# The adaLN block with attention and Fourier branches: the residual gate's products gathered in the branch projection, its rows on GpSimd's queue, value products a step later, the latents' combinations after the modulation

## The chip, the cores and the metric

The kernel runs on one NeuronCore of one Trainium2 chip, as one program. The metric is the time of one execution on the device in microseconds, as the median of several runs. The engines are named TensorE (PE, with its weight loads as PEld), VectorE (DVE), ScalarE (ACT), GpSimd (POOL) and SyncE (SP). SP does no arithmetic here: its queue issues most of the loads. ACT and POOL issue transfers of their own from the queues in which their arithmetic stands, in order: what waits at the head of a queue holds back everything behind it.

## The reference

One layer of a diffusion block over 512 latent tokens of width 2048 and 256 context tokens. A conditioning vector c gives shift, scale and gate through one matrix w_ada; the normed latents are modulated with shift and scale; one wide projection w_in gives queries, keys, values, the input of a Fourier mixer, and four sets of gates; the two branches are projected, weighted with sigmoid gates, summed, projected by w_out, and added to the latents under the residual gate.

```python
shift, scale, gate = jnp.split(silu_c @ w_ada[l] + b_ada[l], 3, axis=-1)
h = _modulate(_rmsnorm(xs, norm_g[l]), shift[:, None], scale[:, None])
p = h @ w_l
q = _rope(_rmsnorm(_heads(p, OFF_Q, N_Q_HEADS), q_norm_g[l]), cos, sin) * q_scale
attn = _attention(q, jnp.concatenate([k, kc], axis=1), jnp.concatenate([v, vc], axis=1))
y_a = (attn * jax.nn.silu(z_a)) @ w_pa
y_b = (_fourier_mix(u_b) * jax.nn.silu(z_b)) @ w_pb
y = (g_a * y_a + g_b * y_b) @ w_o
new_xs = xs + gate[:, None] * y
return _rmsnorm(xs, final_g)
```

There are 12 query heads and 4 key/value heads of 128, 768 keys, and everything is float32. The residual gate is the last third of w_ada: 2048 by 2048 numbers, 16 MB, of which each is used once.

## The kernel before, in words

**Products in three parts.** A float32 operand is split into a high part (ACT copies it to fp32r, L141) and a low part (DVE subtracts, L142). mm3 (L266) makes a product of three matmuls: high by high, high by low, low by high (L268 to L270). Weights come as pieces of 128 x 1024 (512 KB): SP loads a raw tile (L177), ACT and DVE split it into whi and wlo, of which three pairs exist, so at most three pieces lie split ahead of TensorE.

**Pieces.** A list `todo` holds all pieces in the order of their use. start_load (L162) takes the first whose raw tiles are free, get (L230) hands a split piece to the products and splits those behind it, split_piece (L207) does the splitting, and, for the large projections, also issues on POOL the accumulating load of the next combination of weights (L224, tiles R).

**Who orders the work.** The code lists the instructions; a planner then fixes the order on each engine's queue before the program runs, by estimated times: on each engine it takes the first instruction in the code's order that is ready by its estimate, so that work that stands later in the code can come earlier in a queue. The helper `issue_after(x)` puts what it encloses behind instruction x on x's engine. Slots (`take`, `give`) are tiles of 4 KB a partition that pass from hand to hand; a transfer into a slot waits for the slot's last reader.

**Stages, in order of time.** The modulation (start to about 178 us): for each of 16 blocks kb of the latents, POOL loads w_ada's shift and scale columns (wa, L390), TensorE multiplies them with the conditioning vector (L474), ACT copies the result (ado, L481), TensorE turns it (L484), DVE makes shift and gain (L490 to L537), and DVE and ACT make the block's high and low parts (make_h, L462 to L464). In between stand matmuls of the first columns of w_in (start_work, L498), whose sums DVE keeps (L506). In the same loop form_row (L546) makes, for each row of blocks j, sums and differences of quadrants of the latents in one tile f (single-buffered) with six small DVE instructions (two at L551, then L554 to L557), and keep_row (L562) writes f to DRAM (f_d) from ACT's queue; the rows are used for a scheme of seven products in place of eight. Row j needs blocks j and j + 8. Then come the Fourier branch (from 201 us on TensorE; its tiles u, fsq, uh take the space of the modulation's tiles), the keys and values, the seven groups of the wide projection, and attention.

**Attention** (about 849 to 1062 us): a loop (L1135) over 48 steps i = 4h + t, h the head, t a block of 128 queries. scores (L1070) makes 128 x 768 scores in PSUM tile x, DVE takes the maximum (L1079), ACT the exponential (L1081) and the scaling of the branch's gate (L1085). turn (L1089) transposes the probabilities of the step before into tp and splits them (pth, ptl). values (L1100) multiplies two steps' probabilities with the values, on odd i from 3 on. load_head (L981) loads the queries of head h + 2 (POOL, from DRAM) and turn_queries (L988) turns and splits those of head h + 1, both at t = 2; get_keys (L985) splits the next keys and values at i = 12g + 8. As filler, products of branch B's projection stand in every step (tile y, L1057).

**The residual gate.** ask_gate (L969) puts a piece of w_ada's gate columns (512 KB, its 1024 rows of c along the free axis) at the head of `todo`; use_gate (L973, L976) multiplies it on DVE with half of the silu of c, spread over all partitions (crow), and sums along the row into one column of gparts. There are 32 pieces, two halves of c by 16 blocks. load_row (L958) loads half of c from ACT's queue, silu_of_row (L962) makes its silu. The first 16 pieces are spread over attention, one in three steps, the other 16 over the steps m of the branch projection. At m = 19 the sums become a column (gcol), which POOL writes to DRAM as a row (gs, L1258); load_rows (L1279) reads it back, spread over the partitions, along with a row of final_g, from ACT's queue (L1282). It is the first job of the output projection.

**The branch projection** (about 1062 to 1215 us): four chunks of 512 columns, each of six steps m of 24 matmuls. The chunks' sums are in PSUM tiles x and y in turn; DVE weights branch B with its sigmoid gate (L1247, the gates loaded by POOL, L1180), and at a chunk's end merges the two (L1261, L1262). turn_merged (L1193, L1199) and form (L1206 to L1213) prepare the output projection's operands as jobs, one a step.

Of the kernel before, what the change touches and what calls it, by code (L numbers as in the profile page):

```python
# [93 lines left out]
def block_kernel(ctx, tc, xT, ctxT, x, c_row, w_ss, w_gate, vecs, qkg, rope, dft_c, dft_s,  # L94
# [111 lines left out]

    def split_piece(e):  # L207
        if e.out is not None or e.kind == "raw":
            return
        raws = [r for _, r in e.raws]  # L210
        src = raws.pop(0) if e.stage is None else chain[e.pc]
        for r in raws:
            nc.vector.tensor_tensor(src, src, r, op=ALU.add)
        if e.off:
            nc.vector.tensor_tensor(src, chain[e.pc], src, op=ALU.subtract)
        hi, lo = e.dst() if e.dst else hl_tiles()
        if isinstance(hi, Halves):
            for k in range(2):
                split_from(src[:, 512 * k : 512 * k + 512].rearrange("p (a c) -> p a c", a=2), hi.parts[k], lo.parts[k])
        else:  # L220
            hi, lo = hi[:, : e.cols], lo[:, : e.cols]
            split_from(src, hi, lo)
        if e.nxt is not None:
            nc.gpsimd.dma_start(chain[e.pc], e.nxt, accum_op=ALU.add)  # L224
# [321 lines left out]
    def form_row(j):  # L546
# [11 lines left out]
        made.append((j, f))  # L558

    made = []  # L560

    def keep_row():  # L562
        j, f = made.pop()
        nc.scalar.dma_start(f_d[:, :, j, :].rearrange("f p c -> p f c"), f)
# [3 lines left out]
    for kb in range(KK):  # L568
# [18 lines left out]
        if kb > 10:  # L587
            keep_row()
        if kb >= 10:
            form_row(kb - 10)  # L590
    for j in (6, 7):
        keep_row()
        form_row(j)
    keep_row()
# [361 lines left out]
    crow = [None]  # L956

    def load_row(half):  # L958
        crow[0] = rp.tile([P, 1024], F32, tag="raw1", bufs=1, name=uid("crow"))
        nc.scalar.dma_start(crow[0], c_row[:, 1024 * half : 1024 * half + 1024].broadcast_to([P, 1024]))  # L960

    def silu_of_row():  # L962

        e = take((1024,))
        nc.scalar.activation(e, crow[0], ACT.Tanh, scale=0.5)
        nc.vector.scalar_tensor_tensor(crow[0], e, 1.0, crow[0], op0=ALU.add, op1=ALU.mult)
# [6 lines left out]
    def use_gate(q):  # L973

        w = get_aside(("gate", q))
        nc.vector.scalar_tensor_tensor(w, w, 0.5, crow[0], op0=ALU.mult, op1=ALU.mult, accum_out=gparts[:, q : q + 1])  # L976
# [57 lines left out]
    load_row(0)  # L1034
# [65 lines left out]
    def values(half):  # L1100
# [8 lines left out]
        if not second:  # L1109
# [4 lines left out]
        if second:  # L1114
# [3 lines left out]
            give(branch.pop(h), qz.pop(h))  # L1118
            if h % GQ == GQ - 1:
                give(*kept.pop(h // GQ))  # L1120
# [61 lines left out]

    m = -1
# [46 lines left out]
    for n, j in enumerate(CHUNKS):  # L1230
# [9 lines left out]
        for pc, t in products(j, accs) if n else first:  # L1240
# [10 lines left out]
            if 3 <= m < 19:  # L1251
                use_gate(KK + m - 3)
            if m < 16:
                ask_gate(KK + m)
            if m == 19:
# [3 lines left out]
                raw_pools.append((rp, 1, "raw1", 1))  # L1259
        for h in range(2):  # L1260
# [18 lines left out]
    def load_rows(g):  # L1279
        for l, src in ((gates, gs.rearrange("(o k) p -> o (k p)", o=1)), (fgs, final_g)):  # L1280
            l[g] = take((2, 512))
            nc.scalar.dma_start(l[g], src[:, 1024 * g : 1024 * g + 1024].broadcast_to([P, 1024]))  # L1282
# [233 lines left out]
```

## Time and profile before

| What | Value |
|---|---|
| Median of 3 runs | 1390.92 us (1390.05 to 1394.07) |
| The profiled execution's own time | 1391.92 us |
| Its span in the profile | 1390.1 us |
| TensorE busy | 1329.1 us, 96% |
| VectorE busy | 983.6 us, 71% |
| ScalarE busy | 674.7 us, 49% |
| GpSimd busy | 136.9 us, 10% |
| Moved by DMA | 294.16 MB, mean 212 GB/s |
| Mean granted TensorE clock | 0.989 |

The profile is one execution. The first part of its page gives each engine's busy time; the second cuts the span in 40 slices of 34.75 us and gives each engine's busy share in tenths. A table by stretches gives, for each stretch, its length and each engine's busy time (with the number of instructions in brackets), then the clock that TensorE was granted, the mean busy share of the 16 DMA engines, and GB/s. A row of the timeline is start, duration, engine, line of the code, operation, tiles written and read, and in brackets how long the engine stood idle before it and what released it. A row of the waits is: who waited for whom, the total in us, how often, the longest. A "q" behind an engine's name (ACTq) is its queue issuing a transfer. Tile names stand without numbers; s is any slot.

### The profile page before, as it was taken

To read this page: it belongs to the slowest core of one execution; us is meant where nothing else is said; L and a number is where in the kernel's file an instruction comes from. 1 tells how busy PE (TensorE), PEld (TensorE's weight loads), DVE (VectorE), ACT (ScalarE), POOL (GpSimd) and SP (SyncE) were. 2 spreads that over 40 slices of the span, in tenths; PEclk is the share of its full clock that TensorE was granted. 3 is DMA by queue.
4 is the path that set the end of the run, shared out by engine and by line. 5 is a ranking of instruction groups with operands and counts; after the bars stand their busy time and mean duration, and the time that the engine had idled before them with its cause. 6 is when DMAs were issued, how large, how long until landed. Compare 5 with 4: busy or idle time off the path is not lost. (4 is left out here: it accounts for less than half of the span.)

```text
span 1390.1 us, 17752 instructions
## 1 busy us (share of the span) xinstructions
PE 1329.1 (96%) x6664; PEld 1079.8 (78%) x6664; DVE 983.6 (71%) x1266; ACT 674.7 (49%) x1036; POOL 136.9 (10%) x188
## 2 busy tenths in 40 slices
PE   7999999999999999999999999899999969999996
PEld 4676788888888888888888887788788748887875
DVE  4776794859888878665666767767666736577777
ACT  5322263447555555545444456666665113354444
POOL 1111000112011211101010100000001000010100
PEclk9999999999999999999999999999999979999999
DMA  9898476859888788878788886424215964378973
GB/s 385 343 365 319 163 231 219 266 179 255 241 224 216 190 249 213 225 267 199 244 191 248 230 247 197 129 62 152 76 31 171 349 206 122 105 159 217 229 213 137
DMA packets 93157, 294.16 MB, mean 212 GB/s; under 512 B 9232, under 2 KB 26128, under 8 KB 88720
## 3 DMA queue, kind: packets, MB, share of 16 engines
q1 hardware_dynamic: 51264, 178.46, 38.5%
q0 software_dynamic: 21168, 91.24, 26.6%
q10 hardware_dynamic: 20640, 23.33, 5.0%
q8 instruction: 52, 0.85, 0.3%
q14 instruction: 33, 0.27, 0.1%
HBM read 265.73 MB, written 27.27 MB: 211 GB/s over the span
## 5 line engine op out<-in xcount | busy, mean ns | idle before, releaser
L141 ACT ACTIVATE whi<-wr 128x1024 fp32r<-128x1024 f32 (+1 forms) x151 | 158.0, 1047 | 234.9 <-PE x L270 74.1
L142 DVE TENSOR_TENSOR wlo<-wr,whi 128x1024 fp32r<-128x1024 f32 (+1 forms) x151 | 181.8, 1207 | 112.1 <-ACT whi L141 111.9
L268 PE MATMUL y<-whi,s 128*128 128x512 f32 x440 | 176.5, 401 | 17.3 <-ACT whi L141 13.0
L269 PE MATMUL x<-wlo,s 128*128 128x512 f32 x476 | 185.8, 390 | 0.6 <-DVE wlo L142 0.5
L268 PE MATMUL x<-whi,s 128*128 128x512 f32 x476 | 186.1, 391 | 0.2 <-ACT s L863 0.2
L270 PE MATMUL x<-whi,s 128*128 128x512 f32 x476 | 185.5, 390 | 0.0
L269 PE MATMUL y<-wlo,s 128*128 128x512 f32 x440 | 173.0, 393 | 2.5 <-DVE wlo L142 2.5
L270 PE MATMUL y<-whi,s 128*128 128x512 f32 x440 | 172.6, 392 | 0.0
L141 ACT ACTIVATE whi<-R 128x1024 fp32r<-128x1024 f32 x96 | 101.5, 1060 | 109.3 <-PE x L270 63.0
L142 DVE TENSOR_TENSOR wlo<-R,whi 128x1024 fp32r<-128x1024 f32 x96 | 116.8, 1221 | 38.8 <-ACT whi L141 38.7
L268 PEld LDWEIGHTS y<-whi,s 128*128 128x128 f32 x440 | 83.3, 189 | 40.5 <-ACT whi L141 13.4
L268 PE MATMUL x<-s,s 128*128 128x512 f32 (+1 forms) x280 | 106.6, 381 | 5.1 <-ACT s L141 4.2
L269 PE MATMUL x<-s,s 128*128 128x512 f32 (+1 forms) x292 | 109.6, 375 | 0.0
L270 PE MATMUL x<-s,s 128*128 128x512 f32 (+1 forms) x292 | 109.4, 375 | 0.0
L269 PEld LDWEIGHTS x<-wlo,s 128*128 128x128 f32 x476 | 89.4, 188 | 19.8 <-DVE wlo L142 1.5
L268 PEld LDWEIGHTS x<-whi,s 128*128 128x128 f32 x476 | 89.4, 188 | 19.1 <-ACT s L863 0.5
L270 PEld LDWEIGHTS x<-whi,s 128*128 128x128 f32 x476 | 89.3, 188 | 18.7
L269 PEld LDWEIGHTS y<-wlo,s 128*128 128x128 f32 x440 | 83.2, 189 | 19.2 <-DVE wlo L142 4.1
L270 PEld LDWEIGHTS y<-whi,s 128*128 128x128 f32 x440 | 83.2, 189 | 17.6
L224 POOL DMA_DIRECT2D R<-in_w_g x56 | 48.7, 875 | 400.0 <-DVE wlo L142 257.3
L141 ACT ACTIVATE s<-wr 128x512 fp32r<-128x512 f32 (+2 forms) x82 | 55.8, 692 | 48.5 <-PE y L270 16.0
L142 DVE TENSOR_TENSOR s<-wr,s 128x512 fp32r<-128x512 f32 (+2 forms) x82 | 61.2, 764 | 23.1 <-ACT s L141 22.6
(282 smaller groups left out, 2640.8 us busy)
## 6 DMA issues: line engine op xcount, KB each, us to landing
wr<-in_w_g SPq DMA_DIRECT2D x112, 512.0 KB, 4.6
wa<-in_w_ss POOLq DMA_DIRECT2D x28, 1024.0 KB, 9.1
R<-in_w_g POOLq DMA_DIRECT2D x56, 512.0 KB, 7.1
wr<-in_w_pab SPq DMA_DIRECT2D x32, 512.0 KB, 4.5
wr<-in_w_gate SPq DMA_DIRECT2D x32, 512.0 KB, 4.1
R<-in_w_g SPq DMA_DIRECT2D x28, 512.0 KB, 4.6
wr<-in_w_kv SPq DMA_DIRECT2D x24, 512.0 KB, 4.2
wr<-in_w_o SPq DMA_DIRECT2D x24, 512.0 KB, 5.3
```

The source lines that it names most:

```text
L141: nc.scalar.activation(hi, src, ACT.Copy)
L142: return nc.vector.tensor_tensor(lo, src, hi.bitcast(F32), op=ALU.subtract)
L224: nc.gpsimd.dma_start(chain[e.pc], e.nxt, accum_op=ALU.add)
L268: nc.tensor.matmul(o, ah, bh, start=start, stop=False, skip_group_check=cont)
L269: nc.tensor.matmul(o, ah, bl, start=False, stop=False, skip_group_check=cont)
L270: nc.tensor.matmul(o, al, bh, start=False, stop=stop, skip_group_check=cont)
```

## The change

Five edits in one diff. The planner is run anew on the whole program.

- The rows' writes: form_row writes f from POOL's queue itself, and keep_row is gone. All eight rows stand behind the loop over kb, each followed by up to six pieces of the remaining start work.
- The residual gate: no piece is asked for in attention. Steps m = 0 to 15 of the branch projection ask for two pieces each, steps 2 to 17 use two each. use_gate's instructions are queued behind the DVE part of the newest split of a weight piece (issue_after on last_split). The column is made at m = 18.
- The rows of c are loaded from POOL's queue: the first half at step 24 of attention, its silu at step 28; the second half into a slot of its own at the start of the branch projection, its silu at m = 2. Both halves are held at once.
- Attention: values at even i from 4 on (a step later), with one more turn of the loop; load_head and turn_queries at t = 1 in place of 2 (a step earlier); get_keys at i = 12g + 10 in place of 12g + 8. The tiles of the head's queries and of a finished key group are given back before the split of the branch's result, no longer after it.
- load_rows issues its two loads from POOL's queue.

```diff
+    last_split = [None]
...
-            split_from(src, hi, lo)
+            last_split[0] = split_from(src, hi, lo)
...
-        made.append((j, f))
-
-    made = []
-
-    def keep_row():
-        j, f = made.pop()
-        nc.scalar.dma_start(f_d[:, :, j, :].rearrange("f p c -> p f c"), f)
+        nc.gpsimd.dma_start(f_d[:, :, j, :].rearrange("f p c -> p f c"), f)
...
-        if kb > 10:
-            keep_row()
-        if kb >= 10:
-            form_row(kb - 10)
-    for j in (6, 7):
-        keep_row()
+    for j in range(8):
         form_row(j)
-    keep_row()
+        for _ in range(6):
+            next(work, None)
     pa.close()
...
-    crow = [None]
+    crow = [None, None]
 
     def load_row(half):
-        crow[0] = rp.tile([P, 1024], F32, tag="raw1", bufs=1, name=uid("crow"))
-        nc.scalar.dma_start(crow[0], c_row[:, 1024 * half : 1024 * half + 1024].broadcast_to([P, 1024]))
+        row = crow[half] = take((1024,)) if half else rp.tile([P, 1024], F32, tag="raw1", bufs=1, name=uid("crow"))
+        nc.gpsimd.dma_start(row, c_row[:, 1024 * half : 1024 * half + 1024].broadcast_to([P, 1024]))
...
-        nc.vector.scalar_tensor_tensor(w, w, 0.5, crow[0], op0=ALU.mult, op1=ALU.mult, accum_out=gparts[:, q : q + 1])
+        with tc.issue_after(last_split[0].ins):
+            nc.vector.scalar_tensor_tensor(w, w, 0.5, crow[q // KK], op0=ALU.mult, op1=ALU.mult,
+                                           accum_out=gparts[:, q : q + 1])
...
-        if not second:
+        if second:
+            give(qz.pop(h))
+            if h % GQ == GQ - 1:
+                give(*kept.pop(h // GQ))
+        else:
             branch[h] = take((2, T))
...
-            give(branch.pop(h), qz.pop(h))
-            if h % GQ == GQ - 1:
-                give(*kept.pop(h // GQ))
+            give(branch.pop(h))
...
-    for i in range(NSTEP + 2):
+    for i in range(NSTEP + 3):
         h, t = divmod(i, 4)
         if i < NSTEP:
-            if t == 2 and h + 2 < NH:
+            if t == 1 and h + 2 < NH:
                 load_head(h + 2)
-            if i == 4:
-                silu_of_row()
-            if i % 12 == 8 and i // 12 + 1 < NKV:
+            if i == 24:
+                load_row(0)
+            elif i == 28:
+                silu_of_row(0)
+            if i % 12 == 10 and i // 12 + 1 < NKV:
                 get_keys(i // 12 + 1)
...
-        if i % 2 == 1 and i >= 3:
-            values((i - 3) // 2)
+        if i % 2 == 0 and i >= 4:
+            values((i - 4) // 2)
         if 1 <= i <= NSTEP:
             turn(i - 1)
-        if i % 3 == 2 and i < NSTEP:
-            if i > 2:
-                use_gate(i // 3 - 1)
-            ask_gate(i // 3)
-        if t == 2 and h + 1 < NH:
+        if t == 1 and h + 1 < NH:
             turn_queries(h + 1, b1())
...
-        if i >= NSTEP - 1:
+        if NSTEP > i - 2 >= NSTEP - 3:
             next(first)
             next(first)
-    use_gate(KK - 1)
-    load_row(1)
-    silu_of_row()
...
+    load_row(1)
     m = -1
...
-            if 3 <= m < 19:
-                use_gate(KK + m - 3)
+            if m == 2:
+                silu_of_row(1)
+            if 2 <= m < 18:
+                for i in range(2):
+                    use_gate(2 * (m - 2) + i)
             if m < 16:
-                ask_gate(KK + m)
-            if m == 19:
+                for i in range(2):
+                    ask_gate(2 * m + i)
+            if m == 18:
...
+                give(crow[1])
...
             l[g] = take((2, 512))
-            nc.scalar.dma_start(l[g], src[:, 1024 * g : 1024 * g + 1024].broadcast_to([P, 1024]))
+            nc.gpsimd.dma_start(l[g], src[:, 1024 * g : 1024 * g + 1024].broadcast_to([P, 1024]))
```

More of the change, by code (lines that the diff above doesn't have):

```diff
@@ L953, in qz_done, with silu_of_row @@
                                 r[:, b])
-    crow = [None]
+    crow = [None, None]
     def load_row(half):
-        crow[0] = rp.tile([P, 1024], F32, tag="raw1", bufs=1, name=uid("crow"))
-        nc.scalar.dma_start(crow[0], c_row[:, 1024 * half : 1024 * half + 1024].broadcast_to([P, 1024]))
[L962 to L966, printed above, removed]
+        row = crow[half] = take((1024,)) if half else rp.tile([P, 1024], F32, tag="raw1", bufs=1, name=uid("crow"))
+        nc.gpsimd.dma_start(row, c_row[:, 1024 * half : 1024 * half + 1024].broadcast_to([P, 1024]))
+    def silu_of_row(half):
+        e, row = take((1024,)), crow[half]
+        nc.scalar.activation(e, row, ACT.Tanh, scale=0.5)
+        nc.vector.scalar_tensor_tensor(row, e, 1.0, row, op0=ALU.add, op1=ALU.mult)
         give(e)
@@ L1033, in block_kernel @@
     assert not any(p[0] is gvp or p[2] == "raw1" for e in ahead for p, _ in e.raws)
-    load_row(0)
     ybs, S = {}, {}
```

## The prediction

> **What bounds the kernel now.** First the page: the busy shares and the slices.
>
> ```profile
> span 1390.1 us, 17752 instructions
> PE 1329.1 (96%) x6664; PEld 1079.8 (78%) x6664; DVE 983.6 (71%) x1266; ACT 674.7 (49%) x1036; POOL 136.9 (10%) x188
> PE   7999999999999999999999999899999969999996
> ```
>
> TensorE is busy 96% of the span, so only its idle time, 1390.1 - 1329.1 = 61 us, can be won or added to. One slice, the 33rd, stands out. Next the table by stretches, with TensorE's busy time first and the granted clock, DMA share and GB/s last.
>
> ```profile
> 125.00:150.00 25.00, 21.20 (x112) 16.34 (x111) 17.19 (x34) 5.00 (x6) 1.06 (x2) 0.93 0.78 295
> 1075.00:1100.00 25.00, 23.83 (x106) 19.39 (x105) 15.53 (x20) 5.30 (x5) 2.11 (x4) 1.00 0.99 381
> 1125.00:1150.00 25.00, 11.53 (x39) 8.61 (x38) 8.21 (x7) 5.92 (x7) 1.20 (x1) 0.66 0.60 165
> 849.00:1062.00 213.00, 199.25 (x1270) 169.57 (x1268) 148.06 (x234) 139.09 (x264) 4.23 (x8) 1.00 0.33 103
> 1141.80:1147.80 6.00, 5.53 (x12) 4.05 (x13) 5.97 (x6) 3.82 (x4) 0.00 (x0) 0.50 0.46 136
> 141.70:152.70 11.00, 11.00 (x48) 8.78 (x50) 7.66 (x15) 1.91 (x3) 0.00 (x0) 0.88 0.49 167
> ```
>
> Three places hold what the diff can reach: one stall near 1130, 13.5 us of idle; one near 139, 3.8 us; and attention, 849 to 1062, where 213.0 - 199.25 = 13.8 us are scattered in pieces. Third, the timeline around the big stall, by engine.
>
> ```profile
> 1125.36 1.20 POOL L1258 DMA_DIRECT2D gs<-gcol  x1 [4.77 <-DVE gcol L1257]
> 1111.57 1.08 ACT L1199 COPY s<-x 128x512 f32<-128x512 f32 x2 [1.22 <-PE x L1193]
> 1139.33 0.33 ACTq L1282 DMA_DIRECT2D s<-gs  x1
> 1139.69 1.07 ACT L1199 COPY s<-x 128x512 f32<-128x512 f32 x2 [27.04 <-DMA gs<-gcol]
> 1140.65 1.07 ACT L141 ACTIVATE whi<-wr 128x1024 fp32r<-128x1024 f32 x1
> 1141.78 0.79 PE L268 MATMUL y<-whi,s 128*128 128x512 f32 x1 [13.01 <-ACT whi L141]
> ```
>
> ScalarE's queue holds the load of the residual gate's row (L1282), which waits for the write of that row to DRAM (L1258, issued at 1125.36, landed 13.9 us later). The load belongs to the output projection's code, whose first accumulating load is issued at 1211.47 (row below), some 72 us later, but it stands in the queue ahead of the splits of the branch projection's weights. ScalarE does nothing for 27.0 us, TensorE uses up the split weights and stops for 13.4 us (0.4 of it counts as the end of a matmul).
>
> **Part 1, the gate's row on GpSimd's queue.** ScalarE no longer waits at L1282: the 13.4 us go. After the stall the granted clock is 0.50 for 6.0 us (row above), which costs 3.0 us more. Sum 16.4, I take **16**. The Trainium skill's "TensorE: Matmul & The Clock Gate" (What's actually happening) has the array throttled by default and released by about 3.4 us of sustained work; an estimate by it is 1.7 us in place of 3.0, and the trace shows a longer slow stretch.
>
> Next: who pays for the wait on GpSimd? Behind L1282 on that queue stand loads of sigmoid gates (L1180) and accumulating weight loads (L224).
>
> ```profile
> 1185.35 0.53 POOL L1180 DMA_DIRECT2D s<-g_d  x1 [29.84 <-DVE s L1262]
> 1211.47 0.88 POOL L224 DMA_DIRECT2D R<-in_w_o  x1 [25.59 <-DVE wlo L142]
> ```
>
> GpSimd has 25 to 30 us between its last issues. The write of the row now comes from step 18 of 24 of the projection (below), 33 us before its end; less 14 us for the landing and 7 for the loads themselves, the row is there 12 us before the projection ends, and L224's first issue is later than that. Nothing is late next; a queue blocked 14 us longer would cost 0 to 2.
>
> **Part 2, the combinations of the latents (form_row, L546).** The rows move behind the modulation loop in the code, and their eight writes go from ScalarE's to GpSimd's queue.
>
> ```profile
> 137.58 0.69 DVE L551 TENSOR_TENSOR f<-s,s 128x512 f32<-128x512 f32 x1 [5.44 <-DMA f_d<-f]
> 140.95 0.37 ACT L481 COPY ado<-pd 128x256 f32<-128x256 f32 x1 [5.90 <-DVE f L557]
> 141.38 0.69 PE L484 MATMUL pd<-ident,ado 128*128 128x128 f32 x2 [3.80 <-ACT ado L481]
> L551 DVE TENSOR_TENSOR f<-s,s x16: 681/692/693, 26.2 to 172.0; 128x512 f32<-128x512 f32 x16
> DMA to landing us min/median/max: 2.9/4.3/9.7
> 177.47 1.06 ACT L141 ACTIVATE fsq<-wr 128x1024 fp32r<-128x1024 f32 x1 [2.49 <-DMA f_d<-f]
> 201.10 0.28 PE L268 MATMUL pb<-fch,uh 128*128 128x256 f32 x1
> ```
>
> The only buffer f is written out (9.7 us), VectorE waits for it, ScalarE's queue waits for VectorE with the write of the next row, and the modulation's copy (L481) waits behind it: TensorE stops 3.8 us. Then the granted clock is 0.88 for 11.0 us: 1.3 more. Both go, 5.1. Against it: the stage that follows begins when the last row has landed (177.47).
>
> ```profile
> R<-in_w_g POOLq DMA_DIRECT2D x56, 512.0 KB, 7.1
> R<-in_w_g SPq DMA_DIRECT2D x28, 512.0 KB, 4.6
> ```
>
> The same 512 KB into the same tiles land 2.5 us later from GpSimd's queue (part of that is the accumulation). The last row then lands near 180. TensorE needs the stage's first tiles at 201.10, and VectorE is busy 23.2 of 25 us there, so 0 to 3 us come back; I take 1.5. Net gain **3.5**. The eight rows' arithmetic itself (2.6 us each) stays on VectorE in any case. "DMA: Bandwidth & Descriptors" of the Trainium skill (SWDGE vs HWDGE vs iDMA) speaks against this edit: a transfer issued by GpSimd has its descriptors written by software into SBUF, which VectorE can lock out, and one issued by ScalarE has not. The rows above agree in sign, and GpSimd's issues stay at 0.53 us under a busy VectorE.
>
> Are the rows really computed later? The first L551 ran at 26.2, though its code stands after the modulation of step 10, near 90: the planner takes what is ready. So I expect the rows where they are, paced by their inputs.
>
> **Part 3, attention.** Sixteen gate products (L976) and their 16 loads leave it; value products, the next head's queries and the keys shift by one or two steps.
>
> ```profile
> L976 DVE SCALAR_TENSOR_TENSOR wr<-wr,crow 128x1024 f32<-128x1024 f32 x17 | 20.8, 1223 | 8.7 <-DMA wr<-in_w_gate 8.7
> PE x L268 <- ACT s L141: 4.2, 5, 1.1
> PE y L269 <- DVE ptl L142: 2.9, 6, 0.8
> PE y L268 <- DVE s L1113: 1.9, 6, 0.6
> PE tp L1093 <- DVE ptl L142: 1.2, 3, 0.8
> ```
>
> VectorE is relieved of 16/17 of 20.8 + 8.7 us of work and waits, 28 us of 213. Scores waiting for split queries (4.2) get one step more, 4.4 us; value products waiting for split probabilities (2.9) likewise. The last two rows shrink only if VectorE's relief reaches them. Bounds: nothing, or all 13.8; below nothing too, since keys are split two steps before use instead of four. I take **6** of 13.8, most of the first two rows.
>
> **Part 4, the branch projection** gets 32 gate products in place of 16, two at a step, pinned behind the newest weight split on VectorE.
>
> ```profile
> 1080.58 1.06 ACT L141 ACTIVATE whi<-wr 128x1024 fp32r<-128x1024 f32 x1 [4.38 <-PE x L270]
> 1086.02 1.06 ACT L141 ACTIVATE whi<-wr 128x1024 fp32r<-128x1024 f32 x1 [4.38 <-PE x L270]
> 1104.83 1.23 DVE L976 SCALAR_TENSOR_TENSOR wr<-wr,crow 128x1024 f32<-128x1024 f32 x1
> 1105.98 1.22 DVE L1262 TENSOR_TENSOR R<-s,R 128x1024 f32<-128x1024 f32 x1
> 1107.12 1.22 DVE L1261 TENSOR_TENSOR s<-x,s 128x1024 f32<-128x1024 f32 x1
> L976 DVE SCALAR_TENSOR_TENSOR wr<-wr,crow 128x1024 f32<-128x1024 f32 x15 | 18.4, 1224 | 9.8 <-DMA wr<-in_w_gate 9.8
> ```
>
> A step is 1086.02 - 1080.58 = 5.44 us, a chunk of six 32.7. VectorE per chunk: 12 products at 1.15 and 6 splits, 2 branch-B and 4 merging products at 1.14, together 27.5, and up to 5 form instructions (5.7): 33.2, as much as there is. DMA per chunk: 12 gate pieces, 6 weight pieces, 4 sigmoid gates of 0.524 MB; at the 381 GB/s that the stretch from 1075 shows, 1.38 us each, 30.3 of 32.7. Both are just enough, and the work is not urgent: three split weights lie ready (two steps, 10.9 us), and a gate piece is asked for two steps ahead. Without that cover: the waits now are 9.8/15 = 0.65 us a product, 12 of them 7.8 a chunk, over two full chunks 15.6, less 10.9 of lead: 5 us. For nothing speaks that the products now run ahead of the splits and that two waits of 1.2 us at splits and merges come from that. I take **0**, bounds -2 and +8. The row's two silu products (L965, L966) stay two.
>
> **Sum**, against the profiled execution's own 1391.92 (1390.1 span, 1.8 around it): 1391.92 - 16 - 3.5 - 6 - 0 = 1366.4, I say **1366**. The runs' median is 1.0 lower, within their spread.
>
> **Rivals.** (a) The projection pays: VectorE or DMA is the bound in chunks 0 to 2, by the waits of 0.65 us. 5 to 8 us back: 1371 to 1375, and with a poor attention 1380. For it: 33.2 of 32.7 us. Against: the lead of two steps, and chunk 3, which has no products.
> (b) Writes from GpSimd's queue land later, the skill's rule: with 2.5 to 5 us more for each of seven rows, VectorE, which idles 7 to 8 of 25 us there, waits up to 35 us more before the single f; the modulation comes late and part 2 gains nothing or loses 5: 1370 to 1375. For it: the loads of the modulation's weights stand on the same queue.
> (c) Slower: the planner keeps the rows behind the modulation, as the code has them. Then eight rows run one after another from 172 on, each 2.6 us of VectorE and a landing of 4.3 to 7.1 in the single buffer, 7 to 10 us, the last landing at 228 to 250 in place of 177.5. The stage that starts at 177.47 has 201.1 - 177.5 = 23.6 us of cover, of which it needs some 10; the rest, 37 to 60 us, is a stall: 1403 to 1426, say 1413. It decides once the last landing is later than about 190. Against: 26.2 above, and L1282, pulled ahead by some 72 us.
> (d) The change does not do what it says: the row's wait on GpSimd's queue holds sigmoid gates or L224, and half or all of the 16 us stay: 1374 to 1382.
>
> **How the numbers follow.** Forecast 62% (1357 to 1374: attention between 13 and nothing, part 2 between 5 and 1), (a) 13%, (b) 9%, (c) 8%, (d) 5%, and 3% for an order of the queues that makes no difference. The range 1354 to 1386 takes in the forecast with its tails, (a), (b) and (d), and leaves out (c) and the 3%, with some tail for what I have not thought of. Faster by over 0.3% (below 1386.7; 0.3% is about what a measurement of this kernel tells from no change): 62 + 13 + 9 + 5, less 4 for tails: 0.85. Same 0.05, slower 0.10.
>
> **What would show it.** Right: no idle slice at 1130; ScalarE without a wait for gs; no 5.9 us wait of L481 for f; PE's wait for "ACT s L141" in attention near zero; L976 only after attention. Wrong: L551 all after 172 and the tile fsq waiting on f_d (c); VectorE's wait for in_w_gate above 15 us with PE waiting for wlo (a); POOL's wait for gs with a late L1180 or L224 (d).

## The result, and the profile after

The changed kernel takes 1356.86 us (median of 4 runs, 1354.84 to 1359.74) beside 1392.49 us of the kernel before on the same chip: a ratio of 0.9744, with a 95% interval of 0.9716 to 0.9773, or 36 us less. The forecast was 1366 with a range of 1354 to 1386: the time lies in the range, 9 us below the forecast, and just under the 1357 to 1374 that the forecast's own 62% had named. The profiled execution is the slowest of the four, 1359.74 us.

The page of the kernel after, its span, TensorE's busy time and TensorE's slices:

```profile
span 1358.0 us, 17733 instructions
PE 1319.7 (97%) x6664; PEld 1078.9 (79%) x6664; DVE 983.8 (72%) x1266; ACT 672.8 (50%) x1036; POOL 145.6 (11%) x202
PE   6999999999999999999999999999999999999996
```

No slice stands out any more: the 33rd had a 6. The same 6664 matmuls have 38.3 us of idle time around them in place of 61, and, which the forecast had not thought of beyond the half clock, 9.4 us less busy time.

To see where it went I cut both traces at the same events: the first maximum of attention (L1079), the last high-by-high matmul of the projection's chunk 0 in tile x, and the first and last one of chunk 2 (chunk 1 is summed in tile y between them). Times in us, one profiled execution each:

| Stage | before | after | difference | forecast |
|---|---|---|---|---|
| start to the first maximum of attention | 850.1 | 852.9 | +2.8 | -3.5 |
| attention and chunk 0 | 246.3 | 232.8 | -13.5 | -6 |
| chunk 1 (with the big stop) | 54.2 | 34.7 | -19.5 | -16 |
| chunk 2 | 34.2 | 34.2 | 0 | 0 |
| from the end of chunk 2 on | 205.2 | 203.3 | -1.9 | 0 |

Rows of the table by stretches of the kernel after: first the place of the old stop of the start, then the two stages that changed.

```profile
125.00:150.00 25.00, 25.00 (x151) 19.11 (x153) 16.90 (x30) 6.56 (x9) 2.77 (x5) 1.00 0.91 342
852.90:1085.70 232.80, 226.11 (x1429) 196.89 (x1428) 152.64 (x229) 147.85 (x276) 10.00 (x19) 1.00 0.28 101
1085.70:1120.40 34.70, 34.70 (x163) 28.91 (x162) 30.54 (x38) 10.21 (x12) 2.11 (x4) 1.00 0.90 332
```

The same two stages of the kernel before:

```profile
850.10:1096.40 246.30, 232.31 (x1429) 196.96 (x1428) 169.83 (x264) 147.92 (x275) 9.49 (x18) 1.00 0.41 135
1096.40:1150.60 54.20, 38.37 (x162) 30.34 (x161) 30.78 (x36) 10.18 (x12) 3.31 (x5) 0.84 0.73 225
```

In chunk 1 TensorE is never idle any more, at full clock, with the DMA engines busy 90% of the time. In attention 1429 matmuls at full clock have 6.7 us of idle time in place of 14.0, and 6.2 us less busy time.

GpSimd's timeline of the kernel after shows the write of the gate's row, its load, and what stands behind it on the queue:

```profile
1166.48 1.20 POOL L1253 DMA_DIRECT2D gs<-gcol  x1 [5.83 <-DVE gcol L1252]
1177.37 0.54 POOL L1278 DMA_DIRECT2D s<-gs  x1 [9.69 <-DMA gs<-gcol]
1181.18 0.88 POOL L226 DMA_DIRECT2D R<-in_w_o  x1 [3.27 <-DVE wlo L142]
```

The wait of 9.69 us is now GpSimd's, and the accumulating load behind it (L226) waits afterwards for VectorE, not for the row. The 32 gate products, in VectorE's groups between 1065 and 1165 us (busy, mean ns, idle time before them):

```profile
L969 DVE SCALAR_TENSOR_TENSOR wr<-wr,crow 128x1024 f32<-128x1024 f32 x16 | 19.0, 1221 | 1.0 <-DMA wr<-in_w_gate 1.0
L969 DVE SCALAR_TENSOR_TENSOR wr<-wr,s 128x1024 f32<-128x1024 f32 x16 | 19.0, 1221 | 0.8 <-DMA wr<-in_w_gate 0.8
```

Twice as many products as before, with 1.8 us of waits in place of 9.8.

### The profile page after: what moved, and what is told of

It is laid out like the page before. It is cut to its first block, busy times and chain, and to the rows that moved or that the text cites. A ratio compares the mean times of both kernels' runs of the same rounds, so it can differ in the third digit from the quotient of the medians.

```text
span 1358.0 us, 17733 instructions
## 1 busy us (share of the span) xinstructions
PE 1319.7 (97%) x6664; PEld 1078.9 (79%) x6664; DVE 983.8 (72%) x1266; ACT 672.8 (50%) x1036; POOL 145.6 (11%) x202
## 5 line engine op out<-in xcount | busy, mean ns | idle before, releaser
L141 ACT ACTIVATE whi<-R 128x1024 fp32r<-128x1024 f32 x96 | 101.5, 1060 | 109.0 <-PE x L272 64.4
L271 PEld LDWEIGHTS y<-wlo,s 128*128 128x128 f32 x440 | 82.7, 188 | 15.2
L226 POOL DMA_DIRECT2D R<-in_w_g x56 | 48.8, 875 | 400.2 <-DVE wlo L142 258.2
```

Of the source, the lines that this page charges most:

```text
L141: nc.scalar.activation(hi, src, ACT.Copy)
L271: nc.tensor.matmul(o, ah, bl, start=False, stop=False, skip_group_check=cont)
```

## The experiments

**Theory at the start.** Each of the four parts removes what the prediction says, and the parts add up. **First rival**, suggested by the two rows above: two paced products at a step bring the gate's column in time, so that the load of the row would stop nobody on either queue; then the queue edit is worth nothing in the changed kernel. **Second rival**, for attention: its gain is VectorE's relief and not the shift of the value products.

All kernels compute the whole reference. Differences in us are the ratio to the kernel before, less one, times 1392.5.

| Kernel | Median us (runs) | Ratio, 95% interval | Difference |
|---|---|---|---|
| after | 1356.86 (4) | 0.9744, 0.9716 to 0.9773 | -35.6 |
| e1: before, load_rows on GpSimd's queue | 1379.09 (6) | 0.9899, 0.9877 to 0.9921 | -14.1 |
| e2: before, the residual gate's part alone | 1368.07 (4) | 0.9825, 0.980 to 0.985 | -24.4 |
| e3: after, load_rows back on ScalarE's | 1356.61 (5) | 0.9744, 0.9719 to 0.9769 | -35.6 |
| e4: before, the attention shift alone | 1377.39 (6) | 0.9894, 0.987 to 0.9919 | -14.8 |
| e8: before, value products a step later | 1380.34 (4) | 0.9904, 0.9888 to 0.992 | -13.4 |
| e10: before, queries turned a step earlier | 1389.3 (12) | 0.9972, 0.996 to 0.9985 | -3.9 |
| e5: before, the rows' part alone | 1390.57 (12) | 0.9981, 0.9968 to 0.9994 | -2.6 |
| e6: after, the rows' part undone | 1359.22 (4) | 0.9751, 0.9733 to 0.9769 | -34.7 |
| e9: after, gate products not pinned | 1370.14 (5) | 0.9821, 0.9803 to 0.984 | -24.9 |
| e12: e9, load_rows on ScalarE's queue | 1378.33 (4) | 0.9891, 0.9871 to 0.9911 | -15.2 |
| e11: after, keys at their old step | 1356.77 (5) | 0.9736, 0.9715 to 0.9757 | -36.8 |
| e13: after, the rows in halves | 1351.12 (5) | 0.969, 0.9667 to 0.9712 | -43.2 |

### e1 and e2: two ways to lose the same stop

e1 is the queue edit alone:

```diff
-            nc.scalar.dma_start(l[g], src[:, 1024 * g : 1024 * g + 1024].broadcast_to([P, 1024]))
+            nc.gpsimd.dma_start(l[g], src[:, 1024 * g : 1024 * g + 1024].broadcast_to([P, 1024]))
```

> The kernel before, with one edit: the two loads of load_rows come from GpSimd's queue. My theory (ScalarE's queue holds the splits back behind the wait for gs, nothing else): TensorE's 13 us stop near 1130 and the half clock after it are gone, about -16 us (ratio about 0.988), and the wait for gs appears on GpSimd without a late sigmoid gate or accumulating load. Rival 1 (the loads behind it on GpSimd take the stall over): VectorE waits at L1247 or L224 is late, half or more of the 16 us stay. Rival 2 (the stall is worth more than its gap, because what follows was put off with it): more than -20 us.

e2 is the residual gate's part alone (the hunks of load_row, silu_of_row, use_gate, last_split and the steps m of the projection); load_rows stays on ScalarE's queue:

```diff
+        with tc.issue_after(last_split[0].ins):
...
-            if i > 2:
-                use_gate(i // 3 - 1)
-            ask_gate(i // 3)
...
+                for i in range(2):
+                    use_gate(2 * (m - 2) + i)
```

> The kernel before, with the residual gate's part of the change alone: 32 products in the branch projection behind the newest split, rows of c from GpSimd's queue, both halves held; attention's steps, form_row and load_rows as before (the row of the gate still on ScalarE's queue). If VectorE's relief is what attention gains from: attention 8 to 12 us shorter, and TensorE in the projection without waits at wlo (3 us). If the shift of the values and queries is what it gains from: attention at most 3 us shorter. On the stall: if the queue is its cause, ScalarE still waits for gs and TensorE still stops, 5 to 16 us; if the early gate products are its cause (the column is made 12 us after ScalarE stands at the load), the stop is nearly gone. Together -10 to -30 us.

e1 gives -14.1, chunk 1 shrinks by 16.8 to 37.4 us at full clock, and TensorE has no stop of more than 1.3 us there. (In e1's profile attention and chunk 0, which the edit doesn't touch, took 2.8 us more than before: VectorE waited 3.3 us for one gate piece near 974, ahead of a step that TensorE needed.) GpSimd's timeline of e1:

```profile
1129.57 1.20 POOL L1258 DMA_DIRECT2D gs<-gcol  x1 [4.64 <-DVE gcol L1257]
1145.18 0.54 POOL L1282 DMA_DIRECT2D s<-gs  x1 [14.41 <-issue]
1145.71 0.53 POOL L1180 DMA_DIRECT2D s<-g_d  x1
```

The queue is held for 14.41 us and a sigmoid gate's load stands behind it; VectorE waits 7.8 us for that gate until 1154.84, TensorE never waits in consequence. That is the prediction's part 1, to the letter. But e2 gives -24.4 with the load still on ScalarE's queue, and there too chunk 1 is 34.7 us with TensorE busy throughout. ScalarE's wait in e2 (who waited for it, total, times, longest):

```profile
ACT whi L141 <- DMA gs<-gcol: 8.0, 1, 8.0
```

It was 27.0 us in the kernel before. A wait of 8.0 us is less than the 10.9 us that two split pieces last. Attention and chunk 0 also fall, to 239.1 us, 7.2 less: between the 8 to 12 that the expectation had for VectorE's relief and the 3 at most for the shift, so neither is the whole of it. Whether the 7.2 come from the products' work or from the waits for their loads, no run separates.

### e3: the queue edit undone in the kernel after

```diff
-            nc.gpsimd.dma_start(l[g], src[:, 1024 * g : 1024 * g + 1024].broadcast_to([P, 1024]))
+            nc.scalar.dma_start(l[g], src[:, 1024 * g : 1024 * g + 1024].broadcast_to([P, 1024]))
```

> The changed kernel, with load_rows back on ScalarE's queue; TensorE's order of instructions is the same in both. Queue theory: ScalarE waits for the landing of gs, some 8 to 10 us, ahead of a weight split, and TensorE stops for the part that the two split pieces do not cover, with half clock after it: 3 to 16 us slower than the changed kernel. Pacing theory: the wait is short enough for the cover of 10.9 us: within 2 us of the changed kernel, and the queue edit was not needed once the products are paced.

1356.61 us, the ratio of the kernel after to the fourth digit. The write in GpSimd's timeline of e3, then the load in ScalarE's:

```profile
1161.88 1.20 POOL L1253 DMA_DIRECT2D gs<-gcol  x1 [5.83 <-DVE gcol L1252]
```

```profile
1173.08 0.33 ACTq L1278 DMA_DIRECT2D s<-gs  x1
1173.51 1.06 ACT L141 ACTIVATE whi<-wr 128x1024 fp32r<-128x1024 f32 x1 [9.50 <-DMA gs<-gcol]
```

ScalarE begins to wait at 1173.51 - 9.50 = 1164.0, 2 us after the write was issued: it waits for the landing and for nothing else, 9.5 us, and TensorE lives on split pieces meanwhile. In the kernel before it began at 1139.69 - 27.04 = 1112.65, 13 us before the write was issued. So the stop had two halves: a load that stood in its queue 13 us before its data was written, and a landing of 14 us. The other kernels with this load on ScalarE's queue show how much of such a wait the split pieces cover. Waits of 27.0 us (before), 25.2 (e8), 25.0 (e4), 24.8 (e5), 24.3 (e10) and 18.4 (e12) left TensorE stops of 13.0, 9.5, 9.6, 10.8, 10.2 and 3.5 us; waits of 9.5 (e3) and 8.0 (e2) left none. The stop is the wait less 14 to 16 us, so the cover was longer than the 10.9 us that the prediction counted. That either half alone would be covered is an estimate from these rows: it would just fit, and no run has a wait between 9.5 and 18.4 us. In the changed kernel the queue edit is worth nothing that the runs can tell: in e3 chunks 1 and 2 take 34.7 and 34.2 us, as in the kernel after.

### e9 and e12: what keeps the column in time

e9 takes the pin off:

```diff
-        with tc.issue_after(last_split[0].ins):
-            nc.vector.scalar_tensor_tensor(w, w, 0.5, crow[q // KK], op0=ALU.mult, op1=ALU.mult,
-                                           accum_out=gparts[:, q : q + 1])
+        nc.vector.scalar_tensor_tensor(w, w, 0.5, crow[q // KK], op0=ALU.mult, op1=ALU.mult, accum_out=gparts[:, q : q + 1])
```

> The changed kernel without the order that puts each gate product behind the newest weight split. If the pin is what keeps the projection free of waits: products run ahead again, VectorE waits for gate pieces ahead of splits and merges, TensorE waits at wlo and the column is early; with load_rows on GpSimd's queue no long stop: +2 to +5 us against the changed kernel. If two products a step are pace enough by the raw tiles that they need: within 1 us of it.

1370.14 us: 13 us over the kernel after, far more than the expectation had. Chunk 1 takes 44.8 us (+10.1), attention with chunk 0 236.6 (+3.8). VectorE's waits in e9 between 1060 and 1165 us, its timeline at one stop, and TensorE's timeline there:

```profile
DVE wr L968 <- DMA wr<-in_w_gate: 12.8, 6, 4.5
DVE wlo L142 <- ACT whi L141: 5.9, 2, 3.3
DVE s L1236 <- DMA s<-g_d: 4.3, 1, 4.3
```

```profile
1117.13 0.08 DVE L968 DVE_READ_ACCUMULATOR wr<-wr,s 128x1 f32 x1
1121.47 1.22 DVE L1236 TENSOR_TENSOR s<-s,s 128x1024 f32<-128x1024 f32 x1 [4.26 <-DMA s<-g_d]
1122.61 1.22 DVE L142 TENSOR_TENSOR wlo<-wr,whi 128x1024 fp32r<-128x1024 f32 x1
```

```profile
1123.88 0.80 PE L271 MATMUL y<-wlo,s 128*128 128x512 f32 x1 [5.01 <-DVE wlo L142]
```

Products run before the splits. A wait of VectorE for a transfer (12.8 us for gate pieces, 4.3 for a sigmoid gate) then stands ahead of the split that TensorE needs: the split of 1122.61 had its input since 1114.3, when ScalarE finished the piece's high part, but its queue is in order. With the pin the split comes first, the waits for gate pieces are 1.8 us in all, and they and the 4.2 us for sigmoid gates fall on work that nobody waits for.

e12 is e9 with load_rows on ScalarE's queue as in e3. It tells whether the pace or merely the number of products a step made e3 harmless.

> The kernel after without the pin of the gate products behind the splits and with the row's load back on ScalarE's queue. Pinned, the queue made no difference. The pacing theory: without the pin VectorE meets waits for gate pieces and the gate column comes later than the planner's estimate, so the load stands at ScalarE ahead of its data, for longer than two split pieces last (10.9 us): a stop of 3 to 12 us beyond the version with no pin and GpSimd's queue (1370), 1373 to 1382. The rival, that two products at a step alone keep the column in time whatever their order: 1370 within 2 us, and ScalarE waits 10 us or less for gs.

1378.33 us, 8 over e9, as the pacing theory has it. GpSimd's row and ScalarE's row:

```profile
1145.46 1.20 POOL L1251 DMA_DIRECT2D gs<-gcol  x1 [29.47 <-DVE gcol L1250]
```

```profile
1155.97 1.07 ACT L1188 COPY s<-y 128x512 f32<-128x512 f32 x2 [18.39 <-DMA gs<-gcol]
```

ScalarE begins to wait at 1137.6, 8 us before the write is issued, TensorE stops 3.5 us for the split behind it, and chunk 2 grows from 34.2 to 40.6 us. So the same two lines of load_rows cost 14 us, 8 us or nothing, by how well VectorE keeps the time that the planner reckoned with. That the planner's estimate leaves out VectorE's waits for pieces is argued from this, not shown.

### e4, e8, e10, e11: the parts of the attention shift

e4 has the whole shift, with no gate product moved. e8 has of it the later value products and the earlier give:

```diff
-    for i in range(NSTEP + 2):
+    for i in range(NSTEP + 3):
...
-        if i % 2 == 1 and i >= 3:
-            values((i - 3) // 2)
+        if i % 2 == 0 and i >= 4:
+            values((i - 4) // 2)
```

> The kernel before, with the steps of attention alone shifted (values a step later, head loads and queries a step earlier, keys two steps later, tiles given back earlier), gate products as before. If the shift is what attention gains from: the waits of scores for split queries (4.2 us) and of value products for split probabilities (2.9 us) are nearly gone, attention 6 to 9 us shorter, and the stall near 1130 stays: -5 to -9 us. If VectorE's relief is the cause: attention at most 3 us shorter, or longer, since sixteen gate products and their waits stay on VectorE.

> The kernel before, with the value products alone a step later (even steps from 4 on, one more turn of the loop, tiles given back earlier); queries, heads and keys as before. The whole shift gave 246.3 to 235.9 us from attention's first maximum to the end of the projection's first chunk. If the value products are the cause: most of these 10 us, and the wait for split probabilities (2.9 us) gone. If the earlier queries are: 3 us or less, and the wait of scores for split queries (4.2 us) stays or grows, since queries and value products now stand in one step and share a PSUM bank. The stop near 1130 stays.

e10 has only the other end, on the kernel before; e11 takes the keys back to their old step in the kernel after:

```diff
-        if t == 2 and h + 1 < NH:
+        if t == 1 and h + 1 < NH:
             turn_queries(h + 1, b1())
```

```diff
-            if i % 12 == 10 and i // 12 + 1 < NKV:
+            if i % 12 == 8 and i // 12 + 1 < NKV:
```

> The kernel before with one edit: the next head's queries are turned at t = 1 of a head in place of t = 2. It parts the attention shift, of which the whole is worth some 15 us and the value products alone some 13. If queries and values are independent gains, this gives 1 to 3 us (ratio 0.998 to 0.999), and TensorE's wait of the scores for the split queries (4.2 us, 5 times in the kernel before) goes. If instead any step of slack in attention heals most of its stops, because the stops pass from one place to the other, it gives 6 us or more (0.996 or less). If the queries are only the place where a late VectorE shows, it gives nothing and the wait returns as one for ptl or for the exponential.

> The kernel after with one edit undone: the next keys are split at step 12g + 8 again, not 12g + 10. No product waits for keys in either trace, so both theories have it at 1357 within 1 us; if the two steps mattered for VectorE's load around them, the stops for ptl and for the exponential (5 us together) change by up to 2 us, to 1355 or 1359.

e4 -14.8, e8 -13.4, e10 -3.9, and e11 the same as the kernel after. Attention and chunk 0: 246.3 us before, 235.9 in e4, 237.7 in e8, 245.4 in e10. e4's gain is well beyond the 5 to 9 us that were expected. The step of the value products is worth 8.6 of e4's 10.4 us in attention; the rest of their gains is in chunk 1, where the stop is shorter (9.6 and 9.5 us). The second rival, that VectorE's relief is the whole gain, is wrong: the shift alone gives 10.4, the relief alone (e2) 7.2, and both together 13.5, less than their sum, so in part they heal the same stops. TensorE's waits between 850 and 1060 us in e4, in the kernel after, and then the scores' wait alone in e8 and in e10 (there from 845 to 1170 us):

```profile
PE tp L1093 <- DVE ptl L142: 3.8, 5, 1.3
PE x L268 <- ACT s L1081: 3.0, 4, 0.8
PE x L268 <- ACT s L141: 1.0, 1, 1.0
```

```profile
PE tp L1086 <- DVE ptl L142: 2.8, 4, 1.0
PE x L270 <- ACT s L1074: 2.2, 3, 0.8
PE x L270 <- ACT s L141: 1.4, 1, 1.4
```

```profile
PE x L268 <- ACT s L141: 4.8, 9, 1.0
```

```profile
PE x L268 <- ACT s L141: 5.4, 8, 1.1
```

The scores' wait for the split queries goes (4.2 to 1.0 us) only where queries and value products have both moved. In e10 it did not go although the queries are turned a step earlier: the expectation was wrong there, and the gain of e10 stands in chunk 1 (50.8 us) and not in attention. Why, the runs don't settle: the profile of e5, whose edit ends at 180 us, has 51.9 us in chunk 1, so a single profile of that stage moves by 2 us or more, and the 3 us that e4, e8 and e10 gain in chunk 1 may be no more than that.

### e5, e6 and e13: the rows of the latents' combinations

e5 is that part alone, e6 the kernel after without it. Both carry the diff's hunks of form_row, keep_row and the loop, forwards and backwards:

```diff
-        if kb > 10:
-            keep_row()
-        if kb >= 10:
-            form_row(kb - 10)
-    for j in (6, 7):
-        keep_row()
+    for j in range(8):
         form_row(j)
```

> The kernel before, with form_row's part alone: the eight rows behind the modulation loop, their writes from GpSimd's queue. My forecast: ScalarE's wait for the row and the 3.8 us stop near 139 with its slower clock are gone, up to 3 us come back at the start of the Fourier stage: -3.5 us, attention begins near 846 to 848 (850.1 before). Rival 1: what the queue releases is lost where the next stage waits for the last row's landing: between -1 and +1, attention begins at 850 to 854 as in the kernels with the rows in place (850.1, 852.5, 853.6, 850.1). Rival 2: rows run only after the loop: +37 us or more.

> The changed kernel with form_row and keep_row as before (rows in the loop, writes from ScalarE's queue). If the rows' edit gains 3.5 us, this is 3 to 4 us slower than the changed kernel, near 1360; if it gains nothing, 1356 to 1358; if it costs, it is the fastest so far, near 1353. Attention and later as in the changed kernel: from attention's first maximum to the end of the projection's first chunk 232.8 us.

e5 gives -2.6 us (-4.5 to -0.8 by its interval); e6 is 1 us above the kernel after by the ratios, within their intervals. A better measure of so small a gain: seven profiles have the old start (before, e1, e2, e4, e6, e8, e10; 850.1 to 853.6 us to the first maximum of attention, mean 852.1) and six the new one (after, e3, e5, e9, e11, e12; 848.0 to 852.9, mean 850.3). So the part is worth about 1.9 us. The two groups overlap: by their spread the gain lies between 0 and 3.8 (an estimate, 95%), so the 3.5 of the forecast is less likely, not excluded. In the kernel after the tile f shows where the gain went, then VectorE's timeline and TensorE's:

```profile
L553 DVE TENSOR_TENSOR f<-s,s x16: 681/692/694, 25.5 to 173.7; 128x512 f32<-128x512 f32 x16
...
  DVE f L553: 11.4, 7
...
DMA to landing us min/median/max: 3.5/5.4/14.7
```

```profile
163.64 0.69 DVE L553 TENSOR_TENSOR f<-s,s 128x512 f32<-128x512 f32 x1 [2.04 <-DMA f_d<-f]
...
168.70 0.75 DVE L464 SCALAR_TENSOR_TENSOR ht<-xt,gain,rx 128x512 f32<-128x512 f32 x1
```

```profile
170.26 0.50 PE L270 MATMUL pb<-s,whi 128*128 128x512 f32 x1 [2.70 <-ACT s L465]
```

The rows run from 25.5 to 173.7, where they ran before. ScalarE no longer waits for f, but the one buffer is still there: VectorE waits for it 11.4 us in 7 waits, and the 2.04 us at 163.64, with the row's own work, stand ahead of the last block's modulation (L464), for whose parts TensorE stops 2.70 us. All six profiles with the new start have this stop, 2.3 to 2.8 us. The wait has moved from ScalarE's queue to VectorE's.

This pointed to a version that might be better than both. A second f does not fit into the space, but a row needs only two tiles of 128 x 512 if its last two combinations are made in place, and three such tiles take the space of f and its helper:

```diff
-        f = pap.tile([P, 4, 256], F32, tag="f4", bufs=1, name=uid("f4"))
-        v = pap.tile([P, 2, 256], F32, tag="f2", bufs=1, name=uid("f2"))
+        f, v = (pap.tile([P, 2, 256], F32, tag="f2", bufs=3, name=uid("f2")) for _ in range(2))
...
-        nc.gpsimd.dma_start(f_d[:, :, j, :].rearrange("f p c -> p f c"), f)
+        nc.gpsimd.dma_start(f_d[0:2, :, j, :].rearrange("f p c -> p f c"), f)
+        nc.gpsimd.dma_start(f_d[2, :, j, :], s2)
+        nc.gpsimd.dma_start(f_d[3, :, j, :], s4)
```

> The kernel after, with the rows of the latents' combinations in halves: a row needs two tiles of 128 x 512 in place of three (its last two combinations are made in place), and three such tiles stand where f and its helper stood, so that a row can begin before the whole of the row before has landed. Three writes a row in place of one. If the single buffer f still costs time in the kernel after (VectorE waits 11.4 us in 7 waits for f's write, and two of them, 2.0 us each, stand ahead of a modulation that TensorE waits 2.7 us for), VectorE's waits for f fall below 5 us and the time by 1 to 4 us, to 1353 to 1356. If the start is bound elsewhere, TensorE's stops only change their place: 1357 within 1 us. If 16 more writes on GpSimd's queue land later than one large one, the stage behind the rows starts later: 1358 to 1361.

1351.12 us, 0.969 of the kernel before (0.9667 to 0.9712), 5.7 us below the kernel after by the medians and 7.5 by the ratios: more than the 1 to 4 that were expected, though VectorE's waits for f are not below 5 us. VectorE's wait for f in e13, and the stretch from 125 to 175 us in e13:

```profile
DVE f L552 <- DMA f_d<-f: 6.5, 4, 3.0
```

```profile
125.00:175.00 50.00, 49.98 (x293) 38.33 (x291) 39.25 (x75) 12.46 (x16) 10.21 (x17) 1.00 0.68 241
```

The same stretch of the kernel after, whose work stands at the same point at 125 us (as many matmuls from 50 us on in both, 552):

```profile
125.00:175.00 50.00, 47.30 (x281) 35.90 (x280) 36.27 (x67) 11.93 (x16) 5.04 (x8) 1.00 0.65 235
```

The waits for f fall from 11.4 to 6.5 us, TensorE's stops in this stretch go (2.7 us of idle to none), 12 more matmuls are done in it, and attention begins at 846.0, earlier than in any other profile here (4.3 us before the mean of the six with the new start). The later stages take what they take in the kernel after (232.7, 34.7, 34.2 and 203.0 us).

The profiles can also be laid side by side by the number of the matmul, since TensorE's order up to attention is the same in e13 and the six with the new start, and differs at 7 places in the others. From the 760th to the 1000th matmul, where the old stop was, the seven profiles with the old start take 4.1 to 8.3 us longer than e13, the six with the new start 0.0 to 0.3. From the 1000th to the 1040th, where the stop behind VectorE's wait for f is, the six take 2.7 to 4.3 us longer than e13. Part of this is the clock: in the kernel after it stayed at 1.00 behind the stop of 2.70 us, in e3 it was 0.59 for 4 us behind one of 2.75.

## Why the prediction was right or wrong, point by point

**Part 1, 16 us: the size was right, the cause was one of two.** Alone the queue edit takes 16.8 us off chunk 1 and 14.1 off the whole (e1), TensorE pays nothing for what stands on GpSimd's queue, and the granted clock of 0.50 behind the stop went with it: chunk 1 runs at 1.00. But the step costed the edit against the kernel before, as if the other parts left the stop as it was. Part 4 removes the same stop by itself (e2), and beside it the queue edit is worth nothing (e3). The sum came out because the stop was counted once; with part 4 costed by itself it would have been counted twice.

**Part 2, 3.5 us: right in sign, about 1.9.** The 5.9 us wait of the copy and its 3.8 us stop are gone, as "both go, 5.1" says. What failed is the list of who is late next: VectorE's own wait for f, quoted in that part, was left out of it, and TensorE's stop behind it gave back 2.7 us in the kernel after and up to 4.3 in the other five profiles with the new start. Rival (b) named this wait. The landings did become later, 5.4 and at most 14.7 us in place of 4.3 and 9.7, in sign as the Trainium skill's "DMA: Bandwidth & Descriptors" (SWDGE vs HWDGE vs iDMA) has it, which gives the faster setup to transfers that ScalarE or SyncE issues. VectorE's wait for f grew by only 0.8 us, from 10.6 (the tile's view of the kernel before) to 11.4, so that rival's price of up to 35 us was far off.

**Part 3, 6 us: the term that was mis-sized, it is 13.5 with chunk 0.** The step's bound was "nothing, or all 13.8", the idle time that the busy column leaves. Idle time did fall by 7.3 us, near the 6 taken, and mostly in the two rows that it named: the scores' wait for split queries fell from 4.2 to 1.4 us, the values' wait for split probabilities from 2.9 to none. But the stage gained nearly as much again out of the busy column. The timeline of TensorE in the kernel before shows how busy time can hide a stop:

```profile
895.74 0.50 PE L268 MATMUL y<-whi,s 128*128 128x512 f32 x1 [0.34 <-DVE s L1113]
896.07 0.39 PE L269 MATMUL y<-wlo,s 128*128 128x512 f32 x1
896.29 0.39 PE L270 MATMUL y<-whi,s 128*128 128x512 f32 x1
897.36 0.33 PE L990 MATMUL y<-ident,s 128*128 128x128 f32 x1 [0.68 <-ACT R L1057]
```

Matmuls of 512 columns start 0.23 us apart when nothing is late, but each is on record for 0.39. When the next one is late, the first 0.16 us of that count as busy: 897.36 is 1.07 us behind its predecessor, 0.84 late, and the profile shows 0.68. The starts give the whole loss, as an estimate from this case's own paces: where nobody waits, the next matmul starts 0.227 us after one of 512 columns, 0.118 after one of 256 and 0.109 after a transpose of 128. At these paces the stage's matmuls need 217 us, so it lost 29 us before and 16 after, 13.5 less, which is the whole difference; the idle column has only 14.0 and 6.7 of it. (In chunk 1 of the kernel after, where TensorE never waits, the same paces leave nothing lost.) So the true upper bound of this part was nearer 29 than 13.8.

**Part 4, 0: it gave 2.7 beside part 1, and alone it would have given part 1's gain as well (e2).** Of chunk 1's 19.5 us 16.8 go with the queue edit alone (e1); the other 2.7 are the small waits for splits and merges (1.6 and 1.2 us before), which the step named and gave nothing for. The bounds were -2 and +8. The reason against a loss, that products no longer run ahead of the splits, was right and undervalued: without the pin it is 13 us (e9) where the step had 5. And a chunk is longer than the step's 32.7 us, for it left out the transposes: at full clock it takes 34.2 to 34.7, of which VectorE is busy 30.5 and 32.7, so VectorE had room. Rival (a) is much like what e9 shows; that e9's 1370 us stands beside its 1371 to 1375 is luck, since e9 loses 13 us where the rival had 5 to 8, from a kernel 9 us below the forecast.

**Rivals (c) and (d)** did not occur: L553 runs from 25.5 on, and L226 is not held by the row.

**The sum again**, with what was measured: 1391.9 - 16.8 - 1.9 - 13.5 - 2.7 - 1.9 (the last stage, which no step had) = 1355.1, beside the median of 1356.9. The profiled execution is longer, for its start is the longest of the six with the new start.

## What to carry to other kernels

A load that waits in an arithmetic engine's queue costs nothing as long as the work split ahead outlasts it. What makes it expensive is standing there before its data is computed, so first look when the wait begins and when the write that it waits for is issued, then decide whether to move the load or to pace the producer, and cost two edits that heal the same stop together. Pin the work that may be late behind the work that another engine needs, and read TensorE's loss from the distances of its starts, for the busy column swallows the first part of every stop. When a wait for a single buffer is moved to another engine, it is still there; writing the row in halves, in the same space, took 5.7 us off a kernel in which the order of the queues had taken 2.

## What the runs showed of the hardware

- The write of the gate's column, 2048 numbers that land as single elements (8 KB), took long in every profile: the load could be issued 14.0 us after it in the kernel before, 10.9 in the kernel after, 11.2 in e3, and 9.5 to 15.6 in all fourteen. A write of 512 KB in rows of 1 KB from the same queue had a median of 5.4 us. The Trainium skill's "DMA: Bandwidth & Descriptors" (Specifications) names 512 B as the least transfer for line rate, and (Anatomy of one DMA) a fixed cost of about 2 us; the trace agrees with the first in kind, and the time is several times the second.
- A short stop of TensorE can cost more than itself: behind a stop of 2.3 to 2.8 us at the same place of six kernels the granted clock stayed at 1.00 in one profile (after) and fell in the other five (0.59 for 4 us in e3).
- The start stage of one and the same code differed by up to 5 us between executions (848.0 to 852.9 in the profiles of six kernels), so a part worth 2 us cannot be read from one profile.
- 24 smaller writes in e13 did not land later than 8 large ones: a median of 5.0 and at most 10.2 us in place of 5.4 and 14.7.
